# A decoder step on one core: page-table registers read in batches of four, first x tiles in column pieces, squares kept behind their chunk

## The chip, the core and the metric

The kernel runs on one NeuronCore of a Trainium2 chip. Its engines work side by side, each through its own queue in order: TensorE (PE, with its weight loads as PEld), VectorE (DVE), ScalarE (ACT), GpSimd (POOL) and SyncE (SP), which here only issues DMA transfers and reads registers. The metric is the device time of one execution in microseconds; lower is better. The kernel before takes 1427.67 us (median of 3 runs, 1425.77 to 1428.07).

## The reference

One inference step of a decoder of one layer, for a prompt of 1024 positions and a group of 8 x 8 sampled positions, with shared weights. All is float32.

```python
def rms_norm(x, g):
    y = xf * lax.rsqrt(jnp.mean(xf * xf, axis=-1, keepdims=True) + EPS)
    return (y * g.astype(jnp.float32)).astype(x.dtype)
...
    h = rms_norm(x, norm_mix)
    z = h @ w_in                    # queries, three K/V pairs, gates, pooling channels u
    ...
    o_att = nsa_fn(q, gates, kvs[0], kvs[1], kvs[2])
    o_pool, pool_state = pool_mix(pool_prev, u, pos0, w_pool, pool_scale)
    x = x + jnp.concatenate([o_att, o_pool], axis=-1) @ w_out
    h = rms_norm(x, norm_ffn)
    gate, up = jnp.split(h @ w_ffn_in, 2, axis=-1)
    x = x + (jax.nn.silu(gate) * up) @ w_ffn_out
```

The attention of the sampled positions reads its past keys and values from a paged cache: `rows = cache[page_table]`, with 8 x 4 page numbers of 0 to 39. Those 32 page numbers are what the change reads at another time.

## The kernel before, in words

Precise products are made of three products of values split into a rounded part and a remainder (`split`, lines 161 to 164: ACT casts, DVE subtracts). The work goes in stages: the norm of x (`norm1`), the projections by `w_in`, attention, and the feed-forward part, which is more than half of the span.

*The norm* takes the 1088 rows in three chunks of three row tiles (`CHUNKS`). For each chunk SP loads three tiles of 128 rows by 1024 columns (line 276). For each of eight column blocks of 128, PE transposes the block of all three tiles into PSUM (285), ACT scales it by the norm's weights `gm` into `h1h` (288), and DVE makes the remainder `h1l` (289). So the first column block needs its part of all three tiles. The factor of each row comes beside that: ACT squares each tile and sums it (298), DVE and ACT make the reciprocal root (`rstd_ops`, 241 to 249), PE spreads it over the partitions (305), ACT copies it to `rB` (307). The products do not wait for the factors; they are multiplied by `rB` when they leave PSUM (`zmul`, 310). Behind the norm its memory goes to the staging tiles of the projections, among them `zs`.

*The projections* are 14 units of 128 columns of `w_in`, in the order of `useq` (119): queries 0, the four pooling units (1304 + 384, + 256, + 128, + 0), then 512, 640, 128, 256, 384, 768, 1024, 896, 1152. `stage_unit` (312) loads the next unit's weights (`win_dma`, issued by SP in line 210, two buffers `wraw`), and for each chunk makes 24 products (line 236); after the first chunk it splits the next unit's weights (`whi`, `wlo`, two buffers each). The pooling results are multiplied by small matrices between the units (`pool_mm`, 389), evicted by ACT and DVE (`oth` in line 399, `otl` in 400) and stored by GpSimd (403). The relative-position bias is prepared alongside (`prep_bias`, 406): a table `bt` is made, ACT sends it to memory once as `bd` (430) and once broadcast to 128 copies of each of 8 rows as `br` (431), and SP reads skewed pieces of both back (439 to 449); a GpSimd copy (451) uses one of them.

*The page numbers* lie in one row on chip (`ptrow`, loaded in line 206). `sample_loads` (1053), which belongs to the attention stage, reads each into a register of SP (1061) and issues the load of that page (1063).

The order on each engine isn't that of the program text. A scheduler goes through all instructions with a model of their times and issues on each engine what is ready, the earlier in the text first. The page reads depend only on `ptrow`, so they were issued long before the attention stage, wherever SP had nothing else ready.

Of the kernel before, what the change touches and what calls it, by code (L numbers as in the profile page):

```python
# [74 lines left out]
class K:  # L75
# [14 lines left out]
    def run(self):  # L90
        self.cst = self.pool("cst")
        wps = ExitStack()
        self.wp = self.pool("wp", 2, stack=wps, side="right")
        self.dr = self.pool("dr", 1, DRAM)
        self.odp = [self.dr.tile([128, 4, NT], F32, name=f"odp{i}") for i in range(2)]
        self.odb = [self.dr.tile([128, 4, 128], F32, name=f"odb{i}") for i in range(8)]
        self.x2p = [self.dr.tile([128, D], F32, name=f"x2p{i}") for i in range(9)]
        self.x2t = [self.dr.tile([128, D], F32, name=f"x2t{i}") for i in range(9)]
        self.hdA = self.dr.tile([128, 8, HT], F32, name="hdA")
        self.hdB = [self.dr.tile([128, 8, n], F32, name=f"hdB{n}_{i}") for i, n in enumerate((160, 128, 128))]  # L100
        self.qd = self.dr.tile([8, 128, H, 128], F32, name="qd")
        self.gd = self.dr.tile([NS, 24], F32, name="gd")
        self.bd = self.dr.tile([H, L1 + L3], F32, name="bd")
        self.br = self.dr.tile([H, 128, 384], F32, name="br")
        self.td = [self.dr.tile([3, 8, 128, HT], F32, name=f"td{g}") for g in range(3)]
        self.tl = self.dr.tile([8, 128, HT], F32, name="tl")
        att = ExitStack()
        self.bp = self.pool("bias", 1, stack=att)
        proj = ExitStack()
        self.psd = self.pool("psd", 4, PSUM, stack=proj)  # L110
        self.pst = self.pool("pst", 4, PSUM, stack=proj)
        h1p = self.pool("h1", 1, stack=proj, side="right")
        self.consts()
        bts = ExitStack()
        self.btp = self.pool("bt", 1, stack=bts)
        with ExitStack() as s:
            self.norm1(self.pool("xn", 1, stack=s, side="right"), h1p)
        self.stg = self.pool("stg", 2, stack=proj, side="right")
        self.useq = [0] + [1304 + 128 * k for k in (3, 2, 1, 0)] + [512, 640, 128, 256, 384, 768, 1024, 896, 1152]
        self.ucur = self.w_split(self.w0)  # L120
        pbs = ExitStack()
        pp = self.pool("pb", 1, stack=pbs)
        self.q_unit(0)
        self.pool_setup(pp)
        bias = self.prep_bias()
        next(bias)
        mm = self.pool_mm(pp)
        for k in (3, 2, 1, 0):
            self.pool_unit(pp, k, (lambda: next(mm)) if k < 2 else None)
            next(bias, None)  # L130
        for _ in range(3):
            next(mm)
        self.gates()
        for _ in mm:
            pass
        pbs.close()
        bts.close()
        with ExitStack() as s:
            cp = self.pool("cp", 1, stack=s)
            self.cmp_units(cp)  # L140
            self.compress_setup(cp)
            cmp = self.compress(cp)
            next(cmp)
            for u in (1, 2, 3):
                self.q_unit(u, lambda: next(cmp))
        self.kvp = self.pool("kv", 1, stack=att)
        self.eps = ExitStack()
        self.ep = self.pool("ep", 1, stack=self.eps)
        self.units = [self.unit(i, g, pp) for i in map(int, '01276543') for g in range(2) for pp in range(2)]
        for n, u in enumerate(self.units):  # L150
            u["n"] = n
        early = self.early()
        self.kv_units(lambda: next(early, None))
        for _ in early:
            pass
        proj.close()
        wps.close()
        self.attention(att)
        self.ffn(att)
# [105 lines left out]
    def norm1(self, p1, h1p):  # L265
        nc, I = self.nc, self.I
        self.h1h = h1p.tile([128, 8, NT], F32R, name="h1h")
        self.h1l = h1p.tile([128, 8, NT], F32R, name="h1l")
        self.rB = h1p.tile([128, NT], F32, name="rB")
        self.w0 = None  # L270
        for c, (c0, n) in enumerate(CHUNKS):
            xs = []
            for jj in range(3):
                src, rows = self.x_src(c * 3 + jj)
                x = p1.tile([128, D], F32, name=f"x{jj}", bufs=2)
                nc.sync.dma_start(x[:rows], src)
                xs.append((x, rows))
            if c == 0:
                nc.sync.dma_start(self.gm, I["norm_mix"][0].rearrange("(k p) -> p k", p=128), allow_slow_non_contiguous=True)
            if c == 1:  # L280
                self.late_consts()
            for k in range(8):
                ps = self.tp()
                for jj, (x, rows) in enumerate(xs):
                    nc.tensor.transpose(ps[:, jj * 128:jj * 128 + rows], x[:rows, k * 128:(k + 1) * 128],
                                        self.ident[:rows, :rows])
                hi, lo = self.h1h[:, k, c0:c0 + n], self.h1l[:, k, c0:c0 + n]
                nc.scalar.activation(hi, ps[:, :n], AF.Copy, scale=self.gm[:, k:k + 1])
                nc.vector.scalar_tensor_tensor(lo, ps[:, :n], self.gm[:, k:k + 1], hi.bitcast(F32),
                                               op0=OP.mult, op1=OP.subtract)  # L290
            if c == 0:
                self.w0 = self.win_dma(0)
            ss = p1.tile([128, 3], F32, name="ss", bufs=2)
            if c == 2:
                nc.vector.memset(ss, 1.0)
            for jj, (x, rows) in enumerate(xs):
                sq = p1.tile([128, D], F32, name="sq", bufs=1)
                nc.scalar.activation(sq[:rows], x[:rows], AF.Square, accum_out=ss[:rows, jj:jj + 1])
            v = p1.tile([128, 3], F32, name="n1v", bufs=2)
            r = p1.tile([128, 3], F32, name="n1r", bufs=2)  # L300
            t = p1.tile([128, 3], F32, name="n1t", bufs=2)
            self.rstd_ops(v, r, t, ss)
            ps = self.tp()
            for jj, (x, rows) in enumerate(xs):
                nc.tensor.transpose(ps[:, jj * 128:jj * 128 + rows], r[:rows, jj:jj + 1].to_broadcast([rows, 128]),
                                    self.ident[:rows, :rows])
            nc.scalar.copy(self.rB[:, c0:c0 + n], ps[:, :n])

    def zmul(self, out, ps, c0, n, rows=128, o=0):
        self.nc.vector.tensor_tensor(out, ps[:rows, o:o + n], self.rB[:rows, c0 + o:c0 + o + n], op=OP.mult)  # L310

    def stage_unit(self, c0col, cb, fill=None):
        assert self.useq.pop(0) == c0col
        wh, wl = self.ucur
        nxt = self.win_dma(self.useq[0]) if self.useq else None
        for c, (c0, n) in enumerate(CHUNKS):
            ps = self.dp()
            self.mm3(ps[:, :n], wh, wl, self.h1h, self.h1l, c0, n)
            cb(c, c0, n, ps)
            if c == 0 and nxt:  # L320
                self.ucur = self.w_split(nxt)
            if fill:
                fill()

# [728 lines left out]
    def sample_loads(self, pr):  # L1053
        nc, I, O, sp = self.nc, self.I, self.O, self.sp
        pages = self.pages = getattr(self, "pages", {})
        for w in range(2):
            for b in (2 * pr, 2 * pr + 1):
                for kb in range(4):
                    if w == 0:
                        t = sp.tile([128, 256], F32, name="pg", bufs=8)  # L1060
                        reg = nc.sync.value_load(self.ptrow[0:1, 4 * b + kb:4 * b + kb + 1], min_val=0, max_val=39)  # L1061
                        src = I["cache_sel"][0].rearrange("n t j g d -> n t (j g d)")[ds(reg, 1)]
                        nc.sync.dma_start(t, src.rearrange("n t c -> (n t) c"))
                    else:
                        t = sp.tile([128, 256], F32, name="pw", bufs=8)
                        nc.sync.dma_start(t, I["state_win"][0, b, 128 * kb:128 * kb + 128].rearrange("t j g d -> t (j g d)"))
                        r0 = 8 if kb == 0 else 0
                        nc.sync.dma_start(
                            O["new_win_sample"][0, b, 128 * kb + r0 - 8:128 * kb + 120].rearrange("t j g d -> t (j g d)"),
                            t[r0:])  # L1070
                    pages[w, b, kb] = t
# [679 lines left out]
```

## Time and profile before

| | |
|---|---|
| profiled execution | 1427.47 us |
| its span (first to last instruction) | 1425.7 us |
| PE busy | 1350.0 us, 95% of the span |
| DVE busy | 976.0 us, 68% |
| ACT busy | 659.6 us, 46% |
| GpSimd busy | 209.5 us, 15% |
| moved by DMA | 172.74 MB, mean 121 GB/s |
| page reads (line 1061) | 32, of 0.262 to 1.969 us each |

Times in the trace are microseconds from the span's start. A row of the timeline has the start, the time taken, the engine, the line, the operation, what is written from what, the shapes and a count; in brackets stands how long the engine had been idle before and what ended that. "SPq" and "ACTq" are instructions that only issue a transfer. The chain of work that ended last is followed back from the last instruction, at each step to what released it.

### The profile page before, as it was taken

To read this page: it belongs to the slowest core of one execution; us is meant where nothing else is said; L and a number is where in the kernel's file an instruction comes from. 1 tells how busy PE (TensorE), PEld (TensorE's weight loads), DVE (VectorE), ACT (ScalarE), POOL (GpSimd) and SP (SyncE) were. 2 spreads that over 40 slices of the span, in tenths; PEclk is the share of its full clock that TensorE was granted. 3 is DMA by queue.
4 is the path that set the end of the run, shared out by engine and by line. 5 is a ranking of instruction groups with operands and counts; after the bars stand their busy time and mean duration, and the time that the engine had idled before them with its cause. 6 is when DMAs were issued, how large, how long until landed. Compare 5 with 4: busy or idle time off the path is not lost.

```text
span 1425.7 us, 25457 instructions
## 1 busy us (share of the span) xinstructions
PE 1350.0 (95%) x9490; PEld 1261.4 (88%) x9490; DVE 976.0 (68%) x2267; ACT 659.6 (46%) x1502; POOL 209.5 (15%) x355
## 2 busy tenths in 40 slices
PE   7979999899999989997799999999999999999995
PEld 6968999778878878875699999999999999999995
DVE  5655877787776688886965556556556575869657
ACT  7322454676565677774533333333333363434222
POOL 0124223332322233331000000000000010100000
PEclk9989999999999999998899999999999999999998
DMA  7457331544435132335232333332233262536125
GB/s 201 92 153 243 98 99 35 160 135 143 144 108 178 52 126 100 102 90 171 65 115 64 100 120 109 121 108 91 77 108 122 89 218 69 192 109 212 48 96 185
DMA packets 160087, 172.74 MB, mean 121 GB/s; under 512 B 19443, under 2 KB 126547, under 8 KB 159187
## 3 DMA queue, kind: packets, MB, share of 16 engines
q1 hardware_dynamic: 147331, 126.21, 29.1%
q0 software_dynamic: 11584, 43.31, 8.9%
q10 hardware_dynamic: 1048, 1.59, 1.0%
q8 instruction: 75, 1.23, 0.4%
q14 instruction: 49, 0.40, 0.1%
HBM read 113.35 MB, written 57.84 MB: 120 GB/s over the span
## 4 chain that ended last, share of the span: by engine, by line
PE 70%; DVE 8%; issue 8%; DMA 5%; SPq 4%; ACT 4%; POOL 1%; DVEq 0%; POOLq 0%; ACTq 0%
PE pq L1405 38%; PE dp L236 7%; PE tp L1013 4%; SPq L1061 3%; PE O L1037 2%; PE dp L1199 2%; PE dp L1201 2%; PE O L1038 2%; PE dp L1200 2%; PE S L924 2%; PE S L925 2%; DMA r<-td 1%; DVE blP L164 1%; PE dp L1156 1%; DVE pl L1022 1%
## 5 line engine op out<-in xcount | busy, mean ns | idle before, releaser
L1405 PE MATMUL pq<-bhP,sh 128*128 128x272 f32 x1232 | 358.1, 291 | 8.3 <-ACT sh L163 4.3
L1405 PE MATMUL pq<-blP,sh 128*128 128x272 f32 x1232 | 358.4, 291 | 4.0 <-DVE blP L164 3.5
L1405 PE MATMUL pq<-bhP,sl 128*128 128x272 f32 x1232 | 356.7, 290 | 1.1 <-DVE sl L164 1.1
L1405 PEld LDWEIGHTS pq<-bhP,sh 128*128 128x128 f32 x1232 | 235.0, 191 | 9.8 <-ACT sh L163 5.0
L1405 PEld LDWEIGHTS pq<-blP,sh 128*128 128x128 f32 x1232 | 234.8, 191 | 4.9 <-DVE blP L164 4.9
L1405 PEld LDWEIGHTS pq<-bhP,sl 128*128 128x128 f32 x1232 | 234.7, 190 | 1.7 <-DVE sl L164 1.7
L1405 PE MATMUL pq<-r,sh 128*128 128x272 f32 x1008 | 191.0, 289 | 3.2 <-DVE blk L1477 3.2
L163 ACT CAST sh<-ws 128x512 fp32r<-128x512 f32 (+1 forms) x136 | 78.7, 583 | 206.9 <-PE pq L1405 139.7
L164 DVE TENSOR_TENSOR sl<-ws,sh 128x512 fp32r<-128x512 f32 (+1 forms) x136 | 86.7, 641 | 126.9 <-ACT sh L163 126.8
L1405 PEld LDWEIGHTS pq<-r,sh 128*128 128x128 f32 x1008 | 157.9, 189 | 4.2 <-ACT r L1594 2.2
L1405 PE MATMUL pq<-r,sl 128*128 128x272 f32 x504 | 143.9, 286 | 0.0
L1022 DVE TENSOR_TENSOR pl<-tp,ph 128x512 fp32r<-128x512 f32 (+8 forms) x168 | 103.6, 621 | 42.0 <-ACT ph L1021 40.7
L163 ACT CAST sh<-wr 128x512 fp32r<-128x512 f32 (+1 forms) x102 | 59.1, 583 | 145.1 <-PE pq L1405 133.9
L1021 ACT CAST ph<-tp 128x512 fp32r<-128x512 f32 (+8 forms) x168 | 88.7, 533 | 65.2 <-PE tp L1013 54.6
L236 PE MATMUL dp<-h1h,whi 128*128 128x384 f32 (+1 forms) x336 | 113.0, 337 | 3.2 <-DVE ue L310 3.2
L236 PE MATMUL dp<-h1l,whi 128*128 128x384 f32 (+1 forms) x336 | 112.1, 334 | 0.0
L236 PE MATMUL dp<-h1h,wlo 128*128 128x384 f32 (+1 forms) x336 | 112.0, 333 | 0.0
L1588 POOL DMA_DIRECT2D r<-td x21 | 15.7, 750 | 605.4 <-PE pq L1405 587.6
L1405 PEld LDWEIGHTS pq<-r,sl 128*128 128x128 f32 x504 | 95.2, 189 | 0.0
L164 DVE TENSOR_TENSOR sl<-wr,sh 128x512 fp32r<-128x512 f32 (+1 forms) x102 | 65.0, 637 | 34.7 <-ACT sh L163 34.6
L1037 PE MATMUL O<-ph,vn 128*128 128x256 f32 x264 | 80.6, 319 | 6.6 <-ACT ph L1021 5.1
L1003 POOL TENSOR_SCALAR pwin<-pwin,r 128x640 f32<-128x640 f32 (+4 forms) x64 | 42.4, 666 | 246.0 <-DVE r L996 114.9
(350 smaller groups left out, 3063.4 us busy)
## 6 DMA issues: line engine op xcount, KB each, us to landing
wr<-in_w_ffn_in SPq DMA_DIRECT2D x44, 512.0 KB
td<-blk SPq DMA_DIRECT2D x18, 1088.0 KB
r<-td POOLq DMA_DIRECT2D x21, 816.0 KB, 6.5
wr<-in_w_ffn_out SPq DMA_DIRECT2D x48, 192.0 KB
wraw<-in_w_in SPq DMA_DIRECT2D x14, 512.0 KB
x<-in_x_prompt SPq DMA_DIRECT2D x8, 512.0 KB
qi<-qd SPq DMA_DIRECT2D x8, 512.0 KB
op<-odp SPq DMA_DIRECT2D x16, 256.0 KB
```

Of the source, the lines that this page charges most:

```text
L163: nc.scalar.copy(hi, src)
L164: nc.vector.tensor_tensor(lo, src, hi.bitcast(F32), op=OP.subtract)
L236: nc.tensor.matmul(ps, w[:, k, :], x, start=(k == 0 and j == 0), stop=(k == kt - 1 and j == 2))
L924: nc.tensor.matmul(S[:, c0:c0 + n], q, kh[:, k0:k0 + n], start=True, stop=False)
L925: nc.tensor.matmul(S[:, c0:c0 + n], q, kl[:, k0:k0 + n], start=False, stop=True)
L1003: nc.gpsimd.tensor_scalar(t, t, r[:, hh, b:b + 1], 1.0, op0=OP.mult, op1=OP.mult)
L1013: nc.tensor.transpose(tp[:kk, 256 * x + 128 * hh:256 * x + 128 * hh + 128], u["P"][hh, b][:, kb * 128:kb * 128 + kk], self.ident)
L1021: nc.scalar.copy(ph[:kk, a:e], tp[:kk, a:e])
L1022: nc.vector.tensor_tensor(pl[:kk, a:e], tp[:kk, a:e], ph[:kk, a:e].bitcast(F32), op=OP.subtract)
L1037: nc.tensor.matmul(o, vv, ph[:kk, cs], start=(2 * t + x == 0), stop=False)
L1061: reg = nc.sync.value_load(self.ptrow[0:1, 4 * b + kb:4 * b + kb + 1], min_val=0, max_val=39)
L1405: nc.tensor.matmul(ps[:, c, :HQ], w[:, k], x[:, k, cs], start=(fresh and k == 0 and j == 0), stop=(k == kt - 1 and j == 2), skip_group_che ...
```

## The change

Three edits. The 32 page numbers are read in eight batches of four: from the fifth unit on, `stage_unit` calls `page_regs` after the split of the next unit's weights. The reads are queued on SP behind the last SP instruction traced so far (`issue_after`), which is the load of those weights; they may be issued no earlier, but nothing says how soon after. `sample_loads` uses the registers then. The x tiles of the first chunk are loaded as nine transfers in place of three: columns 0 to 255 of the three tiles, then 256 to 511, then 512 to 1023. And each square of the norm is held behind the ACT instruction before it in the text (`keep_in_program_order`): the first of a chunk behind that chunk's eighth `h1h`, the next ones behind the square before. What comes later in the text is not held behind the squares.

```diff
@@ run
         self.stg = self.pool("stg", 2, stack=proj, side="right")
+        self.pregs = []
@@ norm1
                 x = p1.tile([128, D], F32, name=f"x{jj}", bufs=2)
-                nc.sync.dma_start(x[:rows], src)
                 xs.append((x, rows))
+                if c:
+                    nc.sync.dma_start(x[:rows], src)
+            if c == 0:
+                for cs in (slice(0, 256), slice(256, 512), slice(512, D)):
+                    for jj in range(3):
+                        nc.sync.dma_start(xs[jj][0][:, cs], self.x_src(jj)[0][:, cs])
...
-                nc.scalar.activation(sq[:rows], x[:rows], AF.Square, accum_out=ss[:rows, jj:jj + 1])
+                self.tc.keep_in_program_order(
+                    nc.scalar.activation(sq[:rows], x[:rows], AF.Square, accum_out=ss[:rows, jj:jj + 1]))
@@ new
+    def page_regs(self, n):
+        nc = self.nc
+        sync = [i for i in nc.cur_bb.bb.instructions if i.engine == mybir.EngineType.SP]
+        with self.tc.issue_after(sync[-1]):
+            for _ in range(min(n, 32 - len(self.pregs))):
+                j = len(self.pregs)
+                self.pregs.append(nc.sync.value_load(self.ptrow[0:1, j:j + 1], min_val=0, max_val=39))
@@ stage_unit
             if c == 0 and nxt:
                 self.ucur = self.w_split(nxt)
+                if len(self.useq) < 10:
+                    self.page_regs(4)
@@ sample_loads
-                        reg = nc.sync.value_load(self.ptrow[0:1, 4 * b + kb:4 * b + kb + 1], min_val=0, max_val=39)
+                        reg = self.pregs[4 * b + kb]
```

## Prediction

> **What bounds the kernel now.** I read the chain of work that ended last first, then the source line that it names on the SP queue, then SP's, ACT's and PE's rows in order of time around it, and the DMA queues in short windows.
>
> ```profile
> PE 70%; DVE 8%; issue 8%; DMA 5%; SPq 4%; ACT 4%; POOL 1%; DVEq 0%; POOLq 0%; ACTq 0%
> ```
> ```profile
> L1061 SPq TENSOR_LOAD <-ptrow x32: 262/688/1969, 38.7 to 83.2; - x32
> ```
>
> PE carries 70% of the chain, so whatever this change is worth must be time in which PE stood or ran slowly. SP's 4% is nearly all line 1061, the 32 page reads, which the scheduler put into one pile from 38.7 to 84.2 us. That a line is on the chain does not say that its time comes back; for that I look at what PE lost, and to whom.
>
> ```profile
> 86.00:106.00 20.00, 11.32 (x50) 9.77 (x51) 13.79 (x23) 6.90 (x14) 6.04 (x11) 0.74 0.61 182
> 140.00:160.00 20.00, 19.90 (x133) 19.29 (x132) 14.76 (x40) 7.79 (x18) 6.00 (x9) 1.00 0.36 118
> ```
> ```profile
> 88.55 0.69 PE L236 MATMUL dp<-plh,wph 128*128 128x384 f32 x1 [2.57 <-DVE otl L400]
> 93.06 0.64 PE L236 MATMUL dp<-h1h,whi 128*128 128x320 f32 x1 [3.18 <-DVE ue L310]
> ```
>
> (Windows: length, then PE, PEld, DVE, ACT, POOL busy with counts, clock, DMA share, GB/s.) From 86 to 106 us PE issued 50 matmuls; undisturbed, from 140 to 160, it issued 133. Fifty would take 50 x 20/133 = 7.5 us, so 12.5 us are lost here, the most that the page reads can be answerable for. They begin with two gaps of 2.57 and 3.18 us, and the granted clock of 0.74 adds to them. The rest of the kernel holds no page read, and its stages simply follow on in time.
>
> **Who causes that hole.** Each gap is a wait for DVE, and DVE waits for ACT:
>
> ```profile
> 48.62 1.28 ACTq L431 DMA_DIRECT2D br<-bt  x1
> 75.02 1.11 ACT L163 CAST plh<-pl 128x1088 fp32r<-128x1088 f32 x1 [2.27 <-DVE pl L379]
> 86.44 1.04 ACT L163 CAST whi<-wraw 128x1024 fp32r<-128x1024 f32 x1 [10.31 <-DMA wraw<-in_w_in]
> 87.39 0.52 ACT L399 ACTIVATE oth<-dp,psc 128x320 fp32r<-128x320 f32 x1
> ```
> ```profile
> 49.50 1.22 DVE L164 TENSOR_TENSOR wlo<-wraw,whi 128x1024 fp32r<-128x1024 f32 x1
> ```
> ```profile
> 50.15 1.97 SPq L1061
> ...
> 63.77 0.39 SPq L210
> ...
> 96.23 4.55 DMA wraw<-in_w_in
> ```
>
> ACT stood 10.31 us for the weight load of column 512, with the pooling product (oth) queued behind it. That load went out at 63.77, in the middle of the pile. Its buffer was free when DVE finished the split at 49.50 + 1.22 = 50.7, so the page reads held it for 13 us. The tempting conclusion is that it would land 13 us sooner. The DMA queues say otherwise (packets, MB, share of 16 engines; q10 carries ACT's broadcast br, q1 SP's loads, q0 GpSimd's stores). First 64 to 68 us, then 68 to 76, then 82 to 87:
>
> ```profile
> q10 hardware_dynamic: 129, 0.20, 43.5%
> q1 hardware_dynamic: 520, 0.26, 25.4%
> ...
> wraw<-in_w_in SPq DMA_DIRECT2D x1, 512.0 KB
> ```
> ```profile
> q10 hardware_dynamic: 258, 0.40, 43.7%
> q0 software_dynamic: 96, 0.30, 9.3%
> ```
> ```profile
> q1 hardware_dynamic: 661, 0.47, 41.2%
> q0 software_dynamic: 128, 0.39, 19.9%
> ```
>
> The broadcast (issued at 48.62) keeps about 7 engines' worth of time (43.7% of 16) busy, on 8 engines it seems. The 512 KB weight load is 1024 packets at the size of these (0.26 MB in 520). About half, 520, pass within 4 us; in the next 8 us q1 moves not one packet, and the other half passes only when the broadcast ends, at about 83 us. GpSimd's stores do the same, with 128 packets left for after it. On the engines that the broadcast holds, everything issued after it waits for its end. A load issued at 50.7 is still issued after it (48.62), so it too would land at about 86. The page reads are slow for that same stretch: 1.97 us each from 50.15.
>
> On this the Trainium skill speaks the other way: DMA: Bandwidth & Descriptors, "Queues, rings and completion order", says that each DMA engine takes turns between the queue rows that have work, a packet at a time. By that rule the load sent at 50.7 would share the engines with the broadcast and be there long before 86. The rows from 68 to 76 do not show such turns, so I follow them.
>
> **The change, part by part.**
>
> *Page reads.* Eight batches of four, each queued on SP behind the weight load of a later unit (512, 640, 128 and so on). The first batch comes at about 51 us under the broadcast; at 1.97 us plus some 0.3 us of register work it takes 4 x 2.3 = 9 us and ends at 60. What stands behind it on SP is the load of bnear (line 439), which reads the broadcast and so can't go before about 83; 23 us cover the batch. The other seven cost 4 x (0.26 to 0.69 + 0.3) = 2 to 4 us each, right behind a weight load, with the next weight load a whole unit of some 12 us away; I put them at 0. If that cover were gone, the price would be those 2 to 4 us at one place, at worst 4. What is gained is at the pile's end:
>
> ```profile
> 84.31 0.37 SPq L439 DMA_DIRECT2D bnear<-br  x1
> ...
> 96.23 2.07 SPq L210 DMA_DIRECT2D wraw<-in_w_in  x2
> ```
> ```profile
> q10 hardware_dynamic: 1048, 1.59, 10.5%
> ```
> ```profile
> 95.82 0.61 POOL L451 COPY bsw<-bss 128x512 f32<-128x512 f32 x1 [7.08 <-DMA bss<-bd]
> ```
>
> SP's bias transfers start at 84.31, just when the reads end, and the weight load of column 640 (96.23, landing 4.55 us later) and the copy for which GpSimd stands 7.08 us hang on them (q10's row is that of the first 135 us, where the broadcast is all but a few of its packets). Without the pile they start when the broadcast's end is reported: at the earliest around 82.5 (its 1048 packets at 129 in 4 us take 32.5, from 48.62 + 1.28 = 49.9), at the latest where they are now. So 0 to 1.8 us; the last packets of q1 and q0 are still pending at 83 to 84, so I take 0.5 us. Then the late column 512 is again what holds PE.
>
> *The first x tiles in column pieces, and the squares.* Both concern the first 36 us, and both act on the same order of ACT's work.
>
> ```profile
> 4.45 0.45 PE L285 MATMUL tp<-ident,x 128*128 128x128 f32 x1 [4.45 <-DMA x<-in_x_prompt]
> 7.73 2.40 PE L285 MATMUL tp<-ident,x 128*128 128x128 f32 x10 [1.48 <-DMA x<-in_x_prompt]
> ```
> ```profile
> 13.29 0.64 PE tp L285 x3
> ...
> 15.52 0.64 PE tp L285 x3
> ```
> ```profile
> L298 ACT ACTIVATE sq<-x x9: 1055/1058/1081, 4.3 to 25.8; 128x1024 f32<-128x1024 f32 x8, 64x1024 f32<-64x1024 f32 x1
> L298 ACT ACTIVATION_READ_ACCUMULATOR sq<-x x9: 185/189/219, 5.3 to 26.8; 128x1 f32 x8, 64x1 f32 x1
> ```
> ```profile
> L276 SPq DMA_DIRECT2D x<-in_x_prompt x8: 340/424/3867, 0.7 to 16.8; - x8
> ```
> ```profile
> 2.60 0.81 SPq L210 DMA_DIRECT2D wraw<-in_w_in  x1
> ```
> ```profile
> 9.27 0.56 ACT L288 ACTIVATE h1h<-tp,gm 128x384 fp32r<-128x384 f32 x1
> ```
> ```profile
> 11.50:16.50 5.00, 5.00 (x22) 4.37 (x21) 4.07 (x7) 3.86 (x8) 0.00 (x0) 1.00 1.04 240
> 16.50:33.70 17.20, 17.16 (x112) 15.15 (x111) 11.11 (x27) 15.01 (x32) 0.00 (x0) 1.00 0.66 146
> ```
>
> Now the first column block is complete only when the third whole tile lands (7.73). With pieces, three column blocks of 256 are on their way after three issues, and PE can transpose from about 4.5 us. It saves the three groups of three transposes that now stand between the first products (from 13.29 to 15.52, 0.64 us each, 1.9 us) and a last 0.3: at most 2.2 us. It does not start the products sooner, since those need the first weight load. That load now leaves SP at 2.60; behind nine pieces (0.42 us an issue) and gm it leaves at about 0.7 + 10 x 0.45 = 5.2. The bytes ahead of it are the same, so I take its landing to move by 0.3 us at most, within ACT's wait for gm.
>
> The squares: three of them, 3 x (1.06 + 0.19) = 3.7 us, now run while ACT has nothing else (from 4.3). Held behind their chunk's last h1h, they go into a stretch where ACT is busy 3.86 of 5.0 and 15.01 of 17.2 us, with 1.1 + 2.2 = 3.3 us free; h1h can start some 0.8 us before 9.27. If all gaps are used the squares cost nothing (3.7 - 3.3 - 0.8 < 0); if none, 3.7 - 0.8 = 2.9 us. Against 2.2 gained, this part lies between -2.2 and +0.7. ACT is nearly as full as PE there, so I take about half of the gain, -1.2 us.
>
> *Sum.* The profiled execution took 1427.47 us (span 1425.7), 0.2 under the median of 1427.67. 1427.47 - 0.5 - 1.2 = 1425.8. The bounds of the same terms are 1427.47 - 1.8 - 2.2 = 1423.5 and 1427.47 + 0.7 = 1428.2. That is my likeliest case and its own range; after the start the shift is carried whole, because br's issue, and with it the hole at 86, moves along with PE.
>
> About 0.2% (2.9 us) is what a measurement of this kernel tells from no change.
>
> **Rivals.**
>
> *The load of column 512 does come early* (the engines take turns after all, or the weight load of 640 gets ahead of the bias transfers). Then both gaps go: 2.57 + 3.18 = 5.75 us, giving 1425.8 - 5.75 = 1420.0, down to 1425.8 - 12.5 = 1413.3 if the whole hole closes. I take the former, because GpSimd still stands until 95.82 for bss with the pooling stores behind it. For it: that load's issue really moves by 13 us, and the chain lies on line 1061. Against it: no q1 packet from 68 to 76. Chance 0.2, all of it faster.
>
> *The squares stop PE* (slower). The norm factors come from the squares, and their broadcast to PSUM (line 305) stands in PE's queue, in order, between products; behind the norm's end stand the first zs on DVE.
>
> ```profile
> 36.09 1.02 DVE L310 TENSOR_TENSOR zs<-dp,rB 128x384 f32<-128x384 f32 x2 [1.49 <-PE tp L305]
> ```
>
> DVE already waited 1.49 us for that. If PE meets line 305 before the squares are done, it stops for up to their 3.7 us; two of three chunks doing so gives 7.4 - 2.2 = +5.2, or 1427.47 - 0.5 + 5.2 = 1432.2. It decides from the point at which ACT's 3.3 us of gaps are not where the squares fall. For it: ACT's 15.01 of 17.2. Against: the order on PE is planned with the squares in their new place. Chance 0.2, of which 0.18 slower by over 0.2%.
>
> *Nothing comes through*: the reads leave SP, the broadcast still ends at 84, and the start's gain is lost again between ACT and DVE: 1427.5. Chance 0.1.
>
> **How the numbers follow.** My case has 0.5; its 1423.5 to 1428.2 crosses the bound of 1424.8, and I give 0.2 of it to faster and 0.3 to same. Faster: 0.2 + 0.2 = 0.40. Same: 0.3 + 0.1 + 0.02 = 0.42. Slower: 0.18. For 8 in 10, the range reaches to 1419 (most of the first rival) and to 1431 (my case, no effect, and the milder part of the squares).
>
> **What would show it.** Right: line 210 for column 512 at about 51 us, yet ACT's whi still waiting to about 85, no q1 packets for some 8 us under q10; bnear between 82 and 84; PE's gaps near 86 to 93 still there; transposes from about 4.5 us with no groups of them between the first products; squares behind each eighth h1h. Wrong: whi of column 512 right behind plh near 76 us (first rival); PE idle before line 305 (second); a different order in the attention stage, which no row here can price.

## The result, and the profile after

| | median us | runs (us) |
|---|---|---|
| before | 1426.72 | 4: 1425.62 to 1428.07 |
| after | 1444.93 | 4: 1443.9 to 1447.81 |

The ratio is 1.0114 (95% interval 1.0091 to 1.0136): the change costs 18 us. The forecast of 1425.8 and its range to 1431 were wrong. The second rival named the mechanism, at half of the price that the squares had (7.4 us; alone they cost 14.8).

The profiled execution of after took 1445.25 us. Its page begins with the span, and the chain of waits has gained in PE (74% for 70%) and lost SP's page reads (SPq 1% for 4%):

```profile
span 1443.5 us, 25458 instructions
...
PE 74%; DVE 8%; DMA 7%; ACT 4%; issue 3%; SPq 1%; POOL 1%; DVEq 0%; POOLq 0%; ACTq 0%
```

So the reads left SP as meant, and the time is not there. Where it goes is seen in windows of the start (length, then PE, PEld, DVE, ACT, POOL busy with counts, granted clock, DMA share, GB/s). First before, then after:

```profile
10.00:20.00 10.00, 9.16 (x49) 8.20 (x49) 7.25 (x15) 8.85 (x17) 0.00 (x0) 1.00 0.93 249
20.00:30.00 10.00, 9.96 (x65) 8.70 (x63) 6.28 (x18) 9.21 (x21) 0.00 (x0) 1.00 0.87 173
30.00:40.00 10.00, 10.00 (x61) 9.17 (x61) 7.65 (x17) 6.81 (x13) 0.55 (x1) 1.00 0.31 67
40.00:50.00 10.00, 10.00 (x60) 8.71 (x59) 6.51 (x15) 2.99 (x9) 4.99 (x10) 1.00 0.52 157
```
```profile
10.00:20.00 10.00, 8.38 (x35) 7.33 (x36) 5.71 (x9) 7.14 (x12) 0.00 (x0) 1.00 0.85 239
20.00:30.00 10.00, 7.48 (x44) 6.89 (x43) 5.58 (x15) 6.96 (x15) 0.00 (x0) 0.83 0.92 249
30.00:40.00 10.00, 6.83 (x29) 4.74 (x28) 3.79 (x10) 6.18 (x13) 0.82 (x4) 0.73 0.22 53
40.00:50.00 10.00, 10.00 (x40) 8.02 (x40) 2.75 (x5) 4.70 (x9) 0.00 (x0) 0.59 0.00 0
```

Two things are to be seen. PE stands: 1.62 + 2.52 + 3.17 = 7.3 us idle in these 40 us, where it was 0.84 + 0.04 = 0.9 before, so 6.4 us more. And PE's clock falls: 0.17 + 0.27 + 0.41 of ten microseconds each, 8.5 us of full clock. An estimate by their sum is 14.9 us. The third row is the plainest: ACT too is *less* busy than before (6.18 for 6.81), so neither engine is the bound; they wait for each other. The chain gives the issue of the broadcast, the marker that ends this stretch:

```profile
63.92 34.86 DMA br<-bt
...
98.80 5.82 DMA bnear<-br
```

It was issued at 48.62 before: 15.3 us later. The first score product of attention stands at 278.5 in place of 261.7, 16.8 us later, the first product of the feed-forward part at 689.0 in place of 671.2, 17.8 us later, and the span is 17.8 us longer. So some 15 of 18 us are lost before any page number is read (the first at 66.7 us), 1.5 more by the first score product, and 1.0 between that and the feed-forward part.

How PE and ACT wait for each other is read from their rows at the second chunk, in order of time:

```profile
17.87 1.05 ACT L305 ACTIVATE sq<-x 128x1024 f32<-128x1024 f32 x1
...
20.23 1.06 ACT L305 ACTIVATE sq<-x 128x1024 f32<-128x1024 f32 x1
...
22.65 0.16 DVE L250 TENSOR_TENSOR n1r<-n1r,n1t 128x3 f32<-128x3 f32 x1
22.96 0.51 PE L312 MATMUL tp<-ident,n1r 128*128 128x128 f32 x3 [2.52 <-DVE n1r L250]
23.31 1.84 PE L291 MATMUL tp<-ident,x 128*128 128x128 f32 x12
...
23.88 2.00 ACT L294 ACTIVATE h1h<-tp,gm 128x384 fp32r<-128x384 f32 x4
...
35.09 0.87 PE L312 MATMUL tp<-ident,n1r 128*128 128x128 f32 x3 [3.17 <-DVE n1r L250]
35.76 3.67 PE L291 MATMUL tp<-ident,x 128*128 128x128 f32 x12
```

(Line 312 of after is the spread of the factors, line 305 of before; 291 are the transposes, 294 is h1h, 305 the squares.) ACT squares three tiles from 17.87 to 21.4, the root takes DVE and ACT to 22.8, and PE's next instruction is the spread that needs it: PE stands 2.52 us. The next chunk's transposes are queued *behind* the spread, so while ACT squares, PE makes nothing for ACT to evict, and then h1h starts only at 23.88. The same comes round at 35.09. Before, the order on PE was the same:

```profile
24.91 0.51 PE L305 MATMUL tp<-ident,n1r 128*128 128x128 f32 x3
25.26 0.82 PE L285 MATMUL tp<-ident,x 128*128 128x128 f32 x6
```

There the spread met factors that were done in time, and it shows no wait: the first chunk's were ready at 10.36 us, long before their spread, the second chunk's at 24.76, only 0.15 us before theirs. They were ready because ACT could put the squares ahead of a chunk's last h1h: the first chunk's ran from 4.34, as each tile came, the second's at 12.74, 17.17 and 20.56, with h1h of that chunk until 23.1. The three spreads began at 16.3, 24.9 and 35.5 us before, at 23.0, 35.1 and 53.4 after.

### The profile page after: what moved, and what is told of

Same layout as the page of the kernel before. It is cut to its first block, busy times and chain, and to the rows that moved or that the text cites. A ratio compares the mean times of both kernels' runs of the same rounds, so it can differ in the third digit from the quotient of the medians.

```text
span 1443.5 us, 25458 instructions
## 1 busy us (share of the span) xinstructions
PE 1363.5 (94%) x9490; PEld 1270.4 (88%) x9490; DVE 977.6 (68%) x2267; ACT 659.5 (46%) x1502; POOL 209.6 (15%) x355
## 4 chain that ended last, share of the span: by engine, by line
PE 74%; DVE 8%; DMA 7%; ACT 4%; issue 3%; SPq 1%; POOL 1%; DVEq 0%; POOLq 0%; ACTq 0%
PE pq L1422 42%; PE dp L237 7%; PE tp L1030 4%; DMA br<-bt 2%; PE O L1054 2%; PE O L1055 2%; PE dp L1216 2%; PE dp L1218 2%; PE dp L1217 2%; PE S L941 2%; PE S L942 2%; DMA r<-td 1%; DMA xr<-in_w_out 1%; DVE blP L165 1%; PE dp L1173 1%
## 5 line engine op out<-in xcount | busy, mean ns | idle before, releaser
L1055 PE MATMUL O<-pl,vn 128*128 128x256 f32 x264 | 79.0, 313 | 0.0
```

Source lines behind the costliest of these rows:

```text
L1055: nc.tensor.matmul(o, vv, pl[:kk, cs], start=False, stop=(2 * t + x == nb - 1))
```

## The experiments

Eight kernels ran. The first four shared one chip, the others another; each ratio is against the kernel before on the same chip (1428.39, then 1427.79).

### One part alone

**The squares alone**, on the kernel before:

```diff
-                nc.scalar.activation(sq[:rows], x[:rows], AF.Square, accum_out=ss[:rows, jj:jj + 1])
+                self.tc.keep_in_program_order(
+                    nc.scalar.activation(sq[:rows], x[:rows], AF.Square, accum_out=ss[:rows, jj:jj + 1]))
```

> The kernel before with the squares held behind their chunk's eighth h1h, and nothing else. Theory A (PE and ACT take turns: the spread of the row factors stands in PE's queue ahead of the next chunk's transposes, so PE waits for the squares and ACT then waits for PE): nearly the whole loss, +12 to +16 us, about 1440 us, with three gaps of PE before line 305 and the issue of br some 13 to 15 us later. Rival B (the nine pieces and the late norm weights and first unit weights do it): at most +3 us here. Rival C (the page reads in batches do it): about 0 here.

Measured: 1443.15 us, ratio 1.0102 (1.0079 to 1.0126). The waits of the first 60 us (engine, tile and line, what it waited for: us in all, times, longest) and a window:

```profile
PE tp L306 <- DVE n1r L249: 6.0, 3, 3.2
...
ACT h1h L288 <- PE tp L285: 13.4, 12, 6.5
```
```profile
30.00:40.00 10.00, 7.35 (x25) 4.70 (x25) 4.79 (x12) 4.30 (x9) 0.82 (x4) 0.59 0.21 53
```

PE waits 6.0 us for the factors at the spread. ACT waits 13.4 us for transposes (2.1 in the kernel before), of which 6.5 lie ahead of the very first h1h, where the squares used to run. So the squares alone bring nearly all of the loss, 14.8 us.

**The page reads alone** (`page_regs`, its call and the use of `pregs`, as in the change):

> The kernel before with the page reads in eight batches, and nothing else. Theory A: 0 to -1.8 us (1425 to 1427), the weight load of column 512 issued near 51 us and still waited for until about 85, because the broadcast br holds its engines. Rival D (the pile of reads made the hole at 86 us): -5.8 to -12.5 us. Rival C: +3 us or more, through the batch that stands ahead of the weight load of column 128.

Measured: 1428.91 us, ratio 1.0001 (0.9987 to 1.0015). Its twelve runs scatter widely (1422.55 to 1432.82), and the profiled one is the fastest of them, so its rows are read for their order, not for the total:

```profile
37.02 12.83 SPq L211 DMA_DIRECT2D wraw<-in_w_in  x2
...
82.11 0.38 SPq L450 DMA_DIRECT2D bnear<-br  x1
```
```profile
81.70 1.05 ACT L164 CAST whi<-wraw 128x1024 fp32r<-128x1024 f32 x1 [6.84 <-DMA wraw<-in_w_in]
```
```profile
q10 hardware_dynamic: 194, 0.30, 43.7%
q1 hardware_dynamic: 7, 0.00, 0.2%
```
```profile
q10 hardware_dynamic: 501, 0.77, 42.8%
q1 hardware_dynamic: 498, 0.25, 5.3%
```

The second of the two weight loads (that of column 512) left SP by 49.9, and ACT still got it only at 81.70, just before the broadcast's end let SP issue bnear (82.11). The last rows are the DMA queues, from 58 to 64 us and from 64 to 80: q10 is the broadcast, q1 has SP's loads. Of the load's 1024 packets about half pass at once (q1 moves 520 from 50 to 54 us), then almost none for ten microseconds, 7 up to 64. From there on q1 moves one packet for each one of the broadcast, 498 beside 501. So the load did not wait for the broadcast's end, but it was done hardly sooner.

**The column pieces alone** (the nine transfers in place of three, as in the change):

> The kernel before with the first x tiles in nine pieces, and nothing else. Theory A: the norm weights and the first unit's weights land about 1 to 2 us later and the squares stand where they stood, so -1 to +2 us. Rival B: +10 us or more. The prediction's term for the pieces: up to -2.2 us.

Measured: 1432.76 us, ratio 1.0022 (1.0008 to 1.0035): slower by itself. ACT in order of time, first before, then this kernel:

```profile
4.34 1.06 ACT L298 ACTIVATE sq<-x 128x1024 f32<-128x1024 f32 x1 [2.10 <-DMA x<-in_x_prompt]
```
```profile
8.51 1.06 ACT L303 ACTIVATE sq<-x 128x1024 f32<-128x1024 f32 x1 [6.27 <-DMA x<-in_x_prompt]
...
11.92 1.51 ACT L293 ACTIVATE h1h<-tp,gm 128x384 fp32r<-128x384 f32 x3
...
15.02 0.67 PE L236 MATMUL dp<-h1h,whi 128*128 128x384 f32 x1
```

A square reads a whole tile. With pieces every tile is complete only when the last pieces land, so ACT's first square starts at 8.51 in place of 4.34, and ACT, which has the squares ahead in its queue, comes to the first h1h at 11.92 (before: 9.27). The first product stands at 15.02. Nothing that PE got earlier reached ACT.

The three single ratios add up to 1.02 + 0.01 + 0.22 = 1.25%, the whole was 1.14 (0.91 to 1.36): within the scatter, the parts account for it.

### Is it the order on PE?

If the loss comes from the spread standing ahead of the next chunk's transposes, moving the spread must give most of it back, with the squares still held. The kernel after, with the spread of a chunk traced behind the next chunk's eight column blocks:

```diff
             self.rstd_ops(v, r, t, ss)
-            ps = self.tp()
-            for jj, (x, rows) in enumerate(xs):
-                nc.tensor.transpose(ps[:, jj * 128:jj * 128 + rows], r[:rows, jj:jj + 1].to_broadcast([rows, 128]),
...
-            nc.scalar.copy(self.rB[:, c0:c0 + n], ps[:, :n])
+            late = (r, xs, c0, n)
+        spread(*late)
...
+            if late:
+                spread(*late)
             if c == 0:
                 self.w0 = self.win_dma(0)
```

(`spread` holds the removed lines.)

> The changed kernel, with the spread of a chunk's row factors (line 312 and the copy to rB) moved in the text behind the next chunk's eight column blocks; the squares stay held. Theory A: PE no longer meets the spread before the squares are done, so at least 10 of the 18 us come back: 1427 to 1434 us, without the gaps before line 312. Rival E (ACT's 3.7 us of squares per chunk are themselves the bound in the first 50 us): at least 1438 us.

Measured: 1435.05 us, ratio 1.0044 (1.0031 to 1.0057): 9.9 us of the 18 come back, just short of the 10 that were expected at the least. The waits of the first 60 us, and the window from 20 to 30:

```profile
PE tp L277 <- DVE n1r L250: 0.9, 1, 0.9
```
```profile
20.00:30.00 10.00, 9.61 (x64) 8.54 (x63) 4.78 (x16) 8.43 (x19) 0.00 (x0) 1.00 0.94 249
```

The wait for the factors fell from 5.9 to 0.9 us, the clock stayed at 1.00, and the broadcast goes out at 52.9 in place of 63.9.

The same without the pieces and the page reads, so the squares held and the spread late on the kernel before:

> The kernel before with the squares held, and the spread of a chunk's row factors behind the next chunk's eight column blocks in the text; no pieces, no batches. Turn-taking of PE and ACT says that most of the 14.5 us of the held squares are gone: +1 to +4 us, the rest being ACT's 3.7 us of squares that lost their free place. If ACT's work is the bound: +8 us or more.

Measured: 1430.98 us, ratio 1.0027 (1.0012 to 1.0041), against 1.0102 with the spread in its old place: about three quarters of the squares' price is the order on PE. Its window from 30 to 40 is where it still loses:

```profile
30.00:40.00 10.00, 8.36 (x51) 7.39 (x49) 5.21 (x16) 6.71 (x13) 0.37 (x2) 1.00 0.32 87
```

1.64 us of PE idle where before had none. The broadcast is issued at 49.67 there, only 1.05 us late. That squares out of their free place cost ACT what is left is argued, not shown. Adding the pieces' 0.22% to this 0.27% gives 0.49%, where the kernel with both (and the page reads) had 0.44%.

### Can the pieces be saved?

One reason for their price might be that gm and the first weights leave later. With pieces alone, `gm` was put ahead of them and the first weight load behind the first three:

```diff
+                nc.sync.dma_start(self.gm, I["norm_mix"][0].rearrange("(k p) -> p k", p=128), allow_slow_non_contiguous=True)
                 for cs in (slice(0, 256), slice(256, 512), slice(512, D)):
                     for jj in range(3):
                         nc.sync.dma_start(xs[jj][0][:, cs], self.x_src(jj)[0][:, cs])
+                    if cs.start == 0:
+                        self.w0 = self.win_dma(0)
```

> The kernel before with the first x tiles in nine pieces, the norm weights gm issued ahead of them and the first unit's weights behind the first three pieces; squares and page reads as before. If the loss of the pieces alone (4 us) comes from the late gm and first weights: 0 to -2 us against before, first product before 11.5 us. If it comes from the pieces themselves or from the order of ACT's squares around them: +2 us or more again.

Measured: 1434.19 us, ratio 1.0045 (1.0031 to 1.0058): no better. It decides nothing about gm, because the scheduler made another order of it:

```profile
7.61 1.04 ACT L163 CAST whi<-wraw 128x1024 fp32r<-128x1024 f32 x1 [5.37 <-DMA wraw<-in_w_in]
8.69 1.22 DVE L164 TENSOR_TENSOR wlo<-wraw,whi 128x1024 fp32r<-128x1024 f32 x1 [6.66 <-ACT whi L163]
9.83 0.22 DVE L181 TENSOR_SCALAR ident<-ii 128x128 f32<-128x128 int32 x1
10.10 3.46 PE L291 MATMUL tp<-ident,x 128*128 128x128 f32 x15 [10.10 <-DVE ident L181]
```

DVE split the weights first and made the identity, which every transpose needs, only then: PE's first transpose comes at 10.10 us. How much of the pieces' price is gm's and the weights' and how much the squares' stays open.

### Who causes the hole at 86 to 106?

The prediction held the broadcast responsible, the first rival the page reads. With the reads alone most of it stayed, even in that kernel's fastest run:

```profile
86.00:106.00 20.00, 12.87 (x60) 10.88 (x61) 13.09 (x24) 6.04 (x10) 6.90 (x14) 0.83 0.62 185
```

60 matmuls, where an undisturbed stretch has 133. The other half of the test is to leave the pile of reads and change the broadcast: made from `bd` in memory, with the 128 copies outermost in place of the 8 rows, and issued by SP. It has to wait for `bd`, whose write is split in two:

```diff
-        self.br = self.dr.tile([H, 128, 384], F32, name="br")
+        self.br = self.dr.tile([128, H, 384], F32, name="br")
...
-        nc.scalar.dma_start(self.bd, bt)
-        nc.scalar.dma_start(self.br[:, :, 0:L1], bt[:, 0:L1].unsqueeze(1).to_broadcast([H, 128, L1]))
+        nc.scalar.dma_start(self.bd[:, 0:L1], bt[:, 0:L1])
+        nc.scalar.dma_start(self.bd[:, L1:], bt[:, L1:])
+        nc.sync.dma_start(self.br[:, :, 0:L1], bass.AP(tensor=self.bd.tensor, offset=self.bd.offset,
+                                                       ap=[[0, 128], [L1 + L3, H], [1, L1]]))
...
-                                  ap=[[383, 128], [128 * 384, H], [1, 256]]))
+                                  ap=[[H * 384 - 1, 128], [384, H], [1, 256]]))
```

> The kernel before, with the broadcast br made from the copy bd in memory, its 128 copies as the outermost dimension, issued by SP, in place of ACT's broadcast from 8 partitions; the page reads stay in their pile. If the broadcast makes the hole at 86 us: q10 no longer holds engines for 33 us, the weight load of column 512 lands within 5 us of its issue, each page read takes 0.3 to 0.7 us, and the time falls by 5 to 12 us (1416 to 1423). If the pile of reads makes it: within 2 us of before.

Measured: 1416.74 us, ratio 0.991 (0.9895 to 0.9926), 11 us faster than before. SP's rows, the reads, the window of the hole, and ACT's wait for weights between 40 and 110 us:

```profile
53.36 0.61 SPq L432 DMA_DIRECT2D br<-bd  x1
...
61.36 0.38 SPq L441 DMA_DIRECT2D bnear<-br  x1
...
69.94 9.71 SPq L210 DMA_DIRECT2D wraw<-in_w_in  x3
```
```profile
L1063 SPq TENSOR_LOAD <-ptrow x32: 262/272/744, 38.5 to 77.6; - x32
```
```profile
86.00:106.00 20.00, 19.01 (x117) 15.71 (x116) 13.91 (x32) 8.68 (x20) 7.31 (x14) 1.00 0.55 175
```
```profile
ACT whi L163 <- DMA wraw<-in_w_in: 2.9, 1, 2.9
```

From the broadcast's issue to the first load that reads it are 8.0 us (35.7 before), though it is issued 4.7 us later; and the hole has 117 matmuls in place of 50, at a clock of 1.00. The page reads are still not in batches (22 from 38.5 us, ten more from 71.0), and the load of column 512 leaves SP at 69.94, even later than before (63.77); yet ACT waits 2.9 us for it in place of 10.31. So a late issue alone makes no hole: the hole was the broadcast's. The reads have a median of 272 ns in place of 688, and none of them falls beside the broadcast. That it is the broadcast which makes them slow is seen best with the reads alone: the four beside it took 1.95 to 2.17 us, the 28 others 0.26 to 0.55. The new broadcast differs in three things at once, its form, its source and its queue; which of them does it was not tested.

With the reads in batches as well:

> The same wide broadcast on the kernel with the page reads in batches. If the broadcast alone makes the hole: within 3 us of the wide broadcast with the pile. If, once the broadcast is out of the way, the pile is what is late next: at least 4 us faster than that one.

Measured: 1415.05 us, ratio 0.992 (0.9907 to 0.9934). The two intervals overlap: with the hole gone, too, it makes no difference that can be told how the page numbers are read. These two kernels beat both kernels of the case.

## Why the prediction was wrong, point by point

**Page reads, taken at -0.5 of 0 to -1.8.** Right in size: alone they give 1.0001 (0.9987 to 1.0015), by which half a microsecond can't be told from nothing. The reason was half right. The weight load of column 512 does leave SP at about 50, and ACT gets it only at 81.70. But that everything issued after the broadcast waits for its end on its engines is not so: after ten microseconds with almost no packet, the load moved packet for packet with it. The kernel before had this too, just behind the rows that the prediction read: from 78 to 82 us q1 moved 116 packets beside 123 of q10. The first rival (the load comes early, 1420.0) is refuted in its time, though the queues do take turns after all; the wide broadcast shows what the hole was worth, 11 us of the 12.5 that the text called the most. Where the Trainium skill (DMA: Bandwidth & Descriptors, "Queues, rings and completion order") lets an engine take turns between queue rows, q1's 498 packets beside 501 of q10 agree, and its 7 beside 194 just before do not; what held the load until then stays open. The same page has a rule with which the trace agrees: in "Rules for kernel authors" it says that an outermost dimension of fewer than 16 keeps the whole transfer on at most so many engines. The broadcast with 8 outermost held 43.7% of 16 engines for 33 us; with 128 outermost, from another source and on another queue, it was through in 8.

**The pieces, taken at up to -2.2 with the first weights "within ACT's wait for gm".** Wrong in sign: alone they cost 0.22%, some 3 to 4 us. The step counted what PE could do earlier and not what ACT has ahead of h1h: whole-tile squares, whose tiles the pieces complete last. In the kernel after, where the squares are held back, gm is what is late: it left SP at 4.98 in place of 2.13, since it too is queued behind the nine pieces, and

```profile
10.08 1.05 ACT L294 ACTIVATE h1h<-tp,gm 128x384 fp32r<-128x384 f32 x2 [7.84 <-DMA gm<-in_norm_mix]
...
12.85 0.69 PE L237 MATMUL dp<-h1h,whi 128*128 128x384 f32 x1
```

The first product stands at 12.85, 1.3 us behind before's:

```profile
11.52 0.67 PE L236 MATMUL dp<-h1h,whi 128*128 128x384 f32 x1
```

The text had put gm's shift at nothing, although it counted gm among the ten issues ahead of the weights.

**The squares, taken at 0 to +2.9 us and absorbed by ACT's gaps.** This is the step that failed: alone they cost 14.8 us. It priced ACT's *room* for 3.7 us of work, and the price was in the *order*: who waits for the result, and what stands behind the waiter. The root hangs on the squares, the spread on the root, the next transposes stand behind the spread on PE, and ACT's next h1h hang on those. So ACT's 3.3 us of gaps were no cover at all; the change made new ones.

**The second rival, 1432.2 at a chance of 0.2.** Its mechanism, place and point were right: PE stops at the spread in two of three chunks, 2.52 + 3.17 us, less than the 3.7 each that it priced. What it left out is the rest. PE's clock falls after these stops and costs about 8.5 us (the estimate above), so that 7.4 for the squares should have been 14.8, and the 2.2 that it took off for the pieces should have been 3 to 4 put on. And what the forecast set against it, "the order on PE is planned with the squares in their new place", did not help: the order after still has the spread in front of the next chunk's transposes, now twelve in a row; how the scheduler's model came to that was not looked into.

**"After the start the shift is carried whole."** Nearly: 15.3 us at the broadcast's issue have become 16.8 at the first score product and 17.8 at the feed-forward part. The hole moved along with it, from 86 to 106 before:

```profile
106.00:126.00 20.00, 14.25 (x67) 11.27 (x67) 11.64 (x21) 5.93 (x10) 7.28 (x14) 0.74 0.61 178
```

The clock there is again 0.74. Which instructions lose the last 2.5 us is not known.

## What to carry to other kernels

Before holding an instruction back, follow its result to the first engine that waits for it in order, and count everything queued behind that wait; free time on the instruction's own engine says nothing about it. When transfers are cut into pieces, ask which readers need the whole tile and which later issues now stand behind more of them. When many queues are late together, look for the one long transfer on their engines before moving what merely waits beside it.

## What the runs showed of the hardware

PE's granted clock falls after a stop, and how long it stays down differs, though the rows show PE busy all the time. After the 2.52 us stop, which ended at 22.96, it was 1.00 until 24, 0.57 from 24 to 28 and 1.00 again from 28 on: 0.83 over ten microseconds is some 3.4 us of half speed. After the 3.17 us stop, which ended at 35.09, three transposes take 0.93 us and a product of 320 columns 0.47, until 48; then it is 0.31 again:

```profile
43.27 0.93 PE L291 MATMUL tp<-ident,x 128*128 128x128 f32 x3
...
47.44 0.47 PE L237 MATMUL dp<-h1h,whi 128*128 128x320 f32 x1
...
48.66 0.31 PE L237 MATMUL dp<-h1h,whi 128*128 128x320 f32 x1
```
```profile
35.00:48.00 13.00, 12.91 (x44) 9.16 (x45) 4.41 (x8) 6.62 (x12) 0.82 (x4) 0.50 0.15 39
```

44 matmuls in 13 us at a clock of 0.50, where before issued 78 at 1.00. The Trainium skill (TensorE: Matmul & The Clock Gate, "What's actually happening") lets the clock fall after an idle window of about 3.4 us and rise after one busy window of that length. Here stops of 2.52 and 3.17 us were enough. The way back fits the page after the first; after the second it took some 13 us of rows that show PE busy.

The clock column does not show all slow time. The first products of both kernels, from 11 to 16 us before and from 12 to 17 after, take 0.5 to 0.7 us (the rows at 11.52 and 12.85 above) where later ones of the same shape take 0.33, and the column reads 1.00 there. The estimate of 8.5 us leaves this out; both kernels have it.

A read of a register from a row on chip takes 0.26 us at the least, and 1.95 to 2.17 beside a transfer that has nothing to do with it (the four reads beside the long broadcast, with the reads alone).
